# A two-layer encoder: all sums of the rope pairs' second-level product on VectorE instead of GpSimd, its inner products in two groups, single units spread between the pairs

## The chip, the cores and the metric

The kernel runs on one core of a Trainium2 chip. The metric is the device time of one execution in microseconds (us), the median of several runs. An engine here is one of TensorE (PE; its weight loads are listed apart as PEld), VectorE (DVE), ScalarE (ACT), GpSimd (POOL) and SyncE (SP), which only issues DMAs. Each engine works through its own queue in order and waits for the others by semaphores.

## What is computed

Two requests of 512 tokens by 1024 channels each go through the same two layers, in float32. Layer 1 is differential attention, layer 2 bidirectional retention; each has one wide input projection (8192 columns in layer 1, 6144 in layer 2), of which the queries and keys are rotated in pairs of columns ("rope"), the values are taken as they are, and a gate goes through SiLU; an output projection ends the layer. Cut to what matters here:

```
def diff_attention(h, w_in, ..., w_out, lambda_init):
    proj = h @ w_in
    q, k, v, gate = jnp.split(proj, [DA_QK_WIDTH, 2 * DA_QK_WIDTH, 2 * DA_QK_WIDTH + D_INNER], axis=-1)
    q = rotary_half(q.reshape(B, S, 2 * N_HEADS, DA_HEAD_DIM)) * (DA_HEAD_DIM ** -0.5)
    k = rotary_half(k.reshape(B, S, 2 * N_HEADS, DA_HEAD_DIM))
    ...
    o = rms_norm(o, subln_g, SUBLN_EPS) * (1.0 - lambda_init)
    o = o.reshape(B, S, D_INNER) * jax.nn.silu(gate)
    return o @ w_out

def trunk(x, ...):
    for i in range(DEPTH):          # 2: attention, then retention
        h = rms_norm(x, norm_g[i], NORM_EPS)
        x = x + (diff_attention(h, ...) if i % 2 == 0 else bidir_retention(h, ...))
    return rms_norm(x, final_norm_g, NORM_EPS)
```

The change touches only the input projections `h @ w_in` of both layers.

## The kernel before

**Split products.** Each operand is split into a high part (a cast on ScalarE, helper `hi_of`, L439) and a low part (a subtraction on VectorE, helper `lo_of`, L442); a product of two operands takes three passes of matmuls (`PASSES`). In the rows of the profile a split of `st` into `ws` is thus one ACT CAST at L439 and one DVE TENSOR_TENSOR at L442.

**Units.** The projection is cut into units of 256 columns, seen as two column halves, two halves of the 1024 input channels, and the two requests. A unit's 2 x 2 x 2 block product is done with seven products P1 to P7 (a Winograd scheme): sums of weight blocks (`combine`, L648) times sums of blocks of the input (`Bop`: B11, B21, B22, T1 to T4, made once per layer by `make_b`). One product is twelve matmuls of 128 x 512 at L712. Results are summed out of PSUM banks (`evac`, sums at L773, copies at L765). A "rope pair" unit is followed by the rotation (`rot_done`); gates are units too, and the values come as "wide" units of twice the width (L722), which hold two `pj` banks and split their last result straight out of them (`os<-pj` at L442). `pj` has three banks.

**Duos.** Two rope units u and v that follow each other share their P2, the product with B21: a `Duo` does it by a second level of the same scheme, over quarter blocks. It has seven inner products of six matmuls of 128 x 256 each (`inner`, L870), into two banks of tag `o`: `yv` and `yu`. Its weight sums s1 to s4 (`put`, L818) and its sums out of the banks (`kept`, L880, behind a ScalarE copy at L879; `added` at L884) are 256 or 512 columns wide. It has four steps, D0 to D3, each with one operand tile in the ring `ws`; the ring has six places, and operands are made ahead as far as the places reach (`projections`). The sums of B21's quarters (`inner_blocks`, L534: t1, t2, t4, t3) are made once per layer. There are twelve duos, eight in layer 1 and four in layer 2.

**Order.** `product_order` lists the products: for a duo, P1 of u, the last product (`tail`) of the unit before, P1 of v, D0, P5 of u, D1, P6, D2, P3, D3, P7, then v's. `mixed` lists the units: two rope units, then a share of the single ones (wides and gates). In layer 1 it makes, after five gates, RR w RR g RR w RR w RR w RR RR RR and two gates, where RR is a duo's two units, w a wide and g a gate. The program is first recorded as operations; `Plan.arrange` then gives each engine its order from estimated costs, and `Plan.issue` writes it out. On the chip that order is fixed.

Of the kernel before, what the change touches and what calls it, by code (L numbers as in the profile page):

```python
# [13 lines left out]
ALU = mybir.AluOpType  # L14
# [3 lines left out]
S = 512  # L18
# [243 lines left out]
def trunk_kernel(  # L262
# [224 lines left out]
    def make_b(layer, source):  # L487
# [37 lines left out]
        def inner_blocks(h):  # L525
# [5 lines left out]
            def block(name, pairs, tile):  # L531
                x = tile
                for j, (a, b) in enumerate(pairs):
                    pool(256, lambda j=j, a=a, b=b: nc.gpsimd.tensor_tensor(x[:, j], a[0](), b[0](), op=ALU.subtract),  # L534
                         [a[1], b[1]], [(x, j)])
                if name != "t3":
                    stored(name, x)
# [52 lines left out]
        for k in range(4):  # L590
            sub(h21[k], h21[k], t[k])
            split("T4", k, *h21[k])
            yield
# [198 lines left out]
    class Duo:  # L792


        n_ws, wide, early = 1, False, None
        STEPS = ("D0", "D1", "D2", "D3")
# [13 lines left out]
        def prep(self, op):  # L810
            u, v = self.u, self.v
# [4 lines left out]
            def put(x, at, a, b, fn, r):  # L816
                out = lambda: four(x[:, at * 256:at * 256 + 256])
                pool(256, lambda: nc.gpsimd.tensor_tensor(out(), a(), b(), op=fn), r, [(x, at)])  # L818
                return out
# [33 lines left out]
        def inner(self, op, n, ps, c0, block, start):  # L853
# [19 lines left out]
            pe(0.681, fn, [w, *bt], [ps])  # L873

        def product(self, op):
            u, v = self.u, self.v

            def kept(e, c, ps, lo, c1):
                act(256, lambda: nc.scalar.copy(e[:, c:c + 256], ps[:, lo:lo + 256]), [ps], [(e, c)])  # L879
                pool(256, lambda: nc.gpsimd.tensor_tensor(  # L880
                    e[:, c:c + 256], e[:, c:c + 256], c1[:, c:c + 256], op=ALU.add), [(e, c), c1], [(e, c)])
# [124 lines left out]
    duos = [0]  # L1006

    def product_order(units, n):
# [14 lines left out]
        duos[0] = 0  # L1023
        while left:
            u = left.pop(0)
            v = left[0] if left else None
            if v and u.kind == v.kind == "pair" and u.done.__qualname__ == v.done.__qualname__:
                left.pop(0)
                d = Duo(u, v)
                duos[0] += 1  # L1030
                out += [(u, "P1"), tail, (v, "P1"), (d, "D0"), (u, "P5"), (d, "D1"), (u, "P6"), (d, "D2"), (u, "P3"),
                        (d, "D3"), (u, "P7"), (v, "P5"), (u, "P4"), (v, "P6"), (v, "P3"), (v, "P7")]
# [191 lines left out]
    def mixed(ropes, gates, wides, n, n_gates):  # L1224
# [173 lines left out]
    step(proj, 7 * len(first_units) + 2 * duos[0] - 6 - 60 - 4)  # L1398
# [201 lines left out]
    step(proj, 7 * len(second_units) + 2 * duos[0] - 10 - 3 - 14)  # L1600
# [270 lines left out]
```

## Time and profile before

| what | value |
|---|---|
| median of 3 runs | 1810.12 us (1809.93 to 1813.53) |
| the profiled execution | 1809.57 us |
| its span, first to last instruction | 1807.8 us |
| granted TensorE clock in it | 0.999 |
| busy share of TensorE / VectorE / ScalarE / GpSimd | 99% / 85% / 51% / 14% |
| HBM traffic | 181 GB/s over the span |

The page gives one line per group of instructions: line, engine, operation, what it writes and reads by the program's names, shape and count, then busy time and mean duration, then the idle time of the engine ahead of it and what ended it. TensorE, VectorE and the rest run beside each other, so a busy share is no bound by itself; the waits of TensorE say where it stood still. By time, the input projection of layer 1 lies between about 45 and 625 us, attention up to 1030, the input projection of layer 2 between about 1110 and 1500, and retention to the end.

### The profile page before, as it was taken

How to read it: one execution, taken by the hardware profiler on the slowest of the kernel's cores; microseconds unless marked ns; L12 is line 12 of the kernel's file. 1: busy time of each engine (PE TensorE's matmuls, PEld its weight loads, DVE VectorE, ACT ScalarE, POOL GpSimd, SP SyncE). 2: the span in 40 equal slices, each digit the busy share in tenths (PEclk: the TensorE clock that was granted, in tenths of full speed). 3: DMA queues.
4: the chain of work that ended last, by engine and by line, in shares of the span. 5: the costliest groups of instructions: out<-in, count | busy, mean ns of one | idle time of the engine just before them, and what ended most of it. 6: DMA issues, size and time to landing. Idle time of an engine off the chain costs nothing.

```text
span 1807.8 us, 28903 instructions
## 1 busy us (share of the span) xinstructions
PE 1781.4 (99%) x10533; PEld 1570.2 (87%) x10533; DVE 1538.0 (85%) x2535; ACT 924.6 (51%) x1988; POOL 245.8 (14%) x356
## 2 busy tenths in 40 slices
PE   9999999999999999999999999999999999999998
PEld 7789889898987888888888878898989998888887
DVE  8978798888799888888888898887988977888887
ACT  8664354444444565554555776444444355444446
POOL 1110110100126011111111211001001000111114
PEclk9999999999999999999999999999999999999999
DMA  6336455463645595544454514473646569664652
GB/s 217 113 112 202 145 174 159 139 195 117 210 121 171 168 350 215 187 187 166 164 188 147 187 65 158 129 233 106 234 133 229 162 203 405 239 239 175 234 209 94
DMA packets 162823, 328.89 MB, mean 182 GB/s; under 512 B 12772, under 2 KB 76920, under 8 KB 162680
## 3 DMA queue, kind: packets, MB, share of 16 engines
q1 hardware_dynamic: 162352, 326.71, 53.1%
q8 instruction: 82, 1.34, 0.3%
q14 instruction: 61, 0.50, 0.1%
q10 hardware_dynamic: 328, 0.34, 0.1%
HBM read 209.55 MB, written 117.44 MB: 181 GB/s over the span
## 4 chain that ended last, share of the span: by engine, by line
PE 85%; DVE 7%; DMA 2%; POOL 2%; issue 1%; ACT 1%; SPq 1%; POOLq 0%; DVEq 0%; ACTq 0%
PE pj L1159 19%; PE pj L712 17%; PE sc L712 10%; PE pj L722 8%; PE o L1487 5%; PE sc L1426 5%; PE o L712 4%; PE sc L722 4%; PE o L870 3%; PE o L1696 2%; PE o L722 2%; DVE ws L442 2%; PE sc L1652 1%; PE tp L1676 1%; PE o L1704 1%
## 5 line engine op out<-in xcount | busy, mean ns | idle before, releaser
L1159 PE MATMUL pj<-ws,arena 128*128 128x512 f32 x1542 | 377.9, 392 | 0.0
L1159 PEld LDWEIGHTS pj<-ws,arena 128*128 128x128 f32 x1542 | 281.8, 188 | 54.6 <-DVE m L988 0.3
L712 PE MATMUL pj<-b,ws 128*128 128x512 f32 x1080 | 263.5, 392 | 1.3 <-DVE b L442 0.7
L439 ACT CAST ws<-st 128x512 fp32r<-128x512 f32 (+1 forms) x260 | 153.3, 601 | 167.1 <-PE o L870 47.5
L712 PEld LDWEIGHTS pj<-b,ws 128*128 128x128 f32 x1080 | 199.4, 188 | 42.2 <-DVE b L442 1.1
L1164 DVE SCALAR_TENSOR_TENSOR b<-pj,pad,b 128x512 f32<-128x512 f32 (+1 forms) x257 | 191.1, 745 | 27.4 <-PE pj L1159 24.3
L442 DVE TENSOR_TENSOR ws<-st,ws 128x512 fp32r<-128x512 f32 (+1 forms) x260 | 176.9, 691 | 41.9 <-ACT ws L439 41.4
L712 PE MATMUL sc<-arena,ws 128*128 128x512 f32 x768 | 186.2, 391 | 0.0
L442 DVE TENSOR_TENSOR ws<-raw,ws 128x512 fp32r<-128x512 f32 (+2 forms) x177 | 143.1, 816 | 31.3 <-ACT ws L439 26.9
L712 PEld LDWEIGHTS sc<-arena,ws 128*128 128x128 f32 x768 | 141.5, 188 | 28.0
L712 PE MATMUL pj<-arena,ws 128*128 128x512 f32 x636 | 156.9, 391 | 7.4 <-DVE os L442 7.4
L712 PEld LDWEIGHTS pj<-arena,ws 128*128 128x128 f32 x636 | 118.1, 188 | 33.2 <-DVE os L442 8.5
L439 ACT CAST ws<-raw 128x512 fp32r<-128x512 f32 (+2 forms) x177 | 124.5, 715 | 29.6 <-PE pj L712 10.3
L1444 ACT ACTIVATE b<-sc,pad 128x512 f32<-128x512 f32 x128 | 87.4, 691 | 72.0 <-DVE pad L1434 71.8
L722 PE MATMUL pj<-ws,b 128*128 128x256 f32 x960 | 116.9, 275 | 0.0
L722 PEld LDWEIGHTS pj<-ws,b 128*128 128x128 f32 x960 | 113.3, 188 | 0.6
L765 ACT COPY c<-pj 128x512 f32<-128x512 f32 x104 | 60.9, 586 | 100.4 <-PE pj L712 62.3
L712 PE MATMUL o<-arena,ws 128*128 128x512 f32 x456 | 108.5, 390 | 3.0 <-DVE b L502 1.8
L712 PEld LDWEIGHTS o<-arena,ws 128*128 128x128 f32 x456 | 85.1, 188 | 21.0 <-ACT ws L439 2.0
L1426 PE MATMUL sc<-arena 128*128 128x512 f32 x384 | 102.0, 398 | 0.7 <-ACT b L1444 0.7
L439 ACT CAST os<-e 128x512 fp32r<-128x512 f32 x96 | 59.1, 621 | 79.6 <-DVE e L773 29.6
L1487 PEld LDWEIGHTS o<-arena 128*128 128x128 f32 x768 | 93.0, 188 | 2.5
(258 smaller groups left out, 3179.0 us busy)
## 6 DMA issues: line engine op xcount, KB each, us to landing
qk<-os SPq DMA_DIRECT2D x192, 256.0 KB, 3.5
arena<-qk SPq DMA_DIRECT2D x96, 512.0 KB, 6.6
v<-os SPq DMA_DIRECT2D x64, 512.0 KB, 4.8
arena<-v SPq DMA_DIRECT2D x64, 512.0 KB, 4.1
raw<-in_da_w_in_dram SPq DMA_DIRECT2D x63, 512.0 KB, 4.2
raw<-in_ret_w_in_dram SPq DMA_DIRECT2D x48, 512.0 KB, 4.3
os<-g SPq DMA_DIRECT2D x32, 512.0 KB, 7.6
g<-e SPq DMA_DIRECT2D x48, 256.0 KB, 3.8
```

What stands on the lines that cost most here:

```text
L439: act(n, lambda: nc.scalar.copy(dst(), src()), r, w)
L442: dve(n, lambda: nc.vector.tensor_tensor(dst(), src(), hi().bitcast(F32), op=ALU.subtract), r, w)
L712: nc.tensor.matmul(ps.t, a[u][0]()[:, k, :], bt[k][:, v, :], start=(opens and k == 0 and i == 0), stop=(k == 3 and i == 2), skip_group_che ...
L722: nc.tensor.matmul(ps[:, (t % 2) * 256:(t % 2) * 256 + 256], bt[k][:, v, t * P:(t + 1) * P], a[u][0]()[:, k, :], start=(opens and t % 2 == ...
L765: act(S, lambda c=c, ps=ps: nc.scalar.copy(c.t, ps.t), [ps], [c])
L870: nc.tensor.matmul(ps[:, c0:c0 + 256], w[:, lo:lo + P], of(b, j), start=(start and j == 0 and i == 0), stop=(j == 1 and i == 2), skip_grou ...
L1159: nc.tensor.matmul(ps[:, here], o[a][:, e, t * P:(t + 1) * P], u[b][:, e, here], start=(m == 0), stop=(m == 5))
L1164: axpy(n, lambda half=half, here=here, ps=ps: nc.vector.scalar_tensor_tensor(half, ps[:, here], rr[:, t % 2:t % 2 + 1], half, op0=ALU.mult ...
L1426: nc.tensor.matmul(s.t, q[:, a, t * P:(t + 1) * P], k[:, b, :], start=(n == 0), stop=(n == 2))
L1444: act(840, lambda j=j, s=s, m=m: nc.scalar.activation(p[:, j, :], s.t, AF.Exp, bias=m.t, accum_out=sm[:, 2 * j + n:2 * j + n + 1]), [s, m] ...
L1487: nc.tensor.matmul(o[:, e * 256:(e + 1) * 256], v[b][:, j, e * P:(e + 1) * P], aT[a][:, j, :], start=(n == 0), stop=(n % 12 == 11), skip_g ...
L1696: nc.tensor.matmul(o[:, e * 256:(e + 1) * 256], v_[v][:, 2 * c + j, e * P:(e + 1) * P], a_[:, u, j * 256:(j + 1) * 256], start=(e == 0 and ...
```

## The change

All second-level sums go from GpSimd to VectorE: the quarter sums of `inner_blocks`, the weight sums `put`, and `kept`, which now adds straight out of the bank instead of a ScalarE copy and a GpSimd sum. T4 is written to the tiles `t` instead of over `h21`, which the quarter sums read. A duo's four steps become two, D1 (with D0's two products) and D3 (with D2's), each taking two places of the ring, D3's group with t3 ahead of b22. The number of single units between the pairs is rounded on the running sum: layer 1 becomes RR w RR g RR RR w RR w RR RR w RR and two gates; layer 2 keeps its order.

```
             def block(name, pairs, tile):
...
-                    pool(256, lambda j=j, a=a, b=b: nc.gpsimd.tensor_tensor(x[:, j], a[0](), b[0](), op=ALU.subtract),
+                    dve(256, lambda j=j, a=a, b=b: nc.vector.tensor_tensor(x[:, j], a[0](), b[0](), op=ALU.subtract),
                          [a[1], b[1]], [(x, j)])
...
         for k in range(4):
-            sub(h21[k], h21[k], t[k])
-            split("T4", k, *h21[k])
+            sub(t[k], h21[k], t[k])
+            split("T4", k, *t[k])
...
     class Duo:
-        n_ws, wide, early = 1, False, None
-        STEPS = ("D0", "D1", "D2", "D3")
+        n_ws, wide, early = 2, False, None
...
         def prep(self, op):
+
+            for part in (("D0", "D1"), ("D2", "D3"))[op == "D3"]:
+                self.part(part)
+
+        def part(self, op):
...
             def put(x, at, a, b, fn, r):
-                pool(256, lambda: nc.gpsimd.tensor_tensor(out(), a(), b(), op=fn), r, [(x, at)])
+                dve(256, lambda: nc.vector.tensor_tensor(out(), a(), b(), op=fn), r, [(x, at)])
...
             def kept(e, c, ps, lo, c1):
-                act(256, lambda: nc.scalar.copy(e[:, c:c + 256], ps[:, lo:lo + 256]), [ps], [(e, c)])
-                pool(256, lambda: nc.gpsimd.tensor_tensor(
-                    e[:, c:c + 256], e[:, c:c + 256], c1[:, c:c + 256], op=ALU.add), [(e, c), c1], [(e, c)])
+                dve(256, lambda: nc.vector.tensor_tensor(
+                    e[:, c:c + 256], ps[:, lo:lo + 256], c1[:, c:c + 256], op=ALU.add), [ps, c1], [(e, c)])
...
-            if op == "D0":
+            if op == "D1":
                 self.yv, self.yu = bank("o"), bank("o")
                 self.eu, self.ev = e_t(), e_t()
-                self.inner(op, 0, self.yv, 0, "b11", True)
+                self.inner("D0", 0, self.yv, 0, "b11", True)
                 kept(self.eu, 0, self.yv, 0, u.s["c1"][0])
-                self.inner(op, 1, self.yu, 0, "b21", True)
-            elif op == "D1":
+                self.inner("D0", 1, self.yu, 0, "b21", True)
                 self.inner(op, 0, self.yu, 256, "t1", False)
                 kept(self.ev, 256, self.yu, 256, v.s["c1"][0])
                 self.inner(op, 1, self.yv, 0, "t2", False)
                 kept(self.eu, 256, self.yv, 0, u.s["c1"][0])
-            elif op == "D2":
-                self.inner(op, 0, self.yu, 256, "b22", False)
-                added(S, self.eu, 0, self.yu, 0, self.eu)
-                u.done(0, 0, [self.eu], u.s, False)
             else:
                 self.inner(op, 0, self.yv, 0, "t3", False)
                 added(256, self.ev, 256, self.yv, 0, self.ev)
+                self.inner("D2", 0, self.yu, 256, "b22", False)
+                added(S, self.eu, 0, self.yu, 0, self.eu)
+                u.done(0, 0, [self.eu], u.s, False)
                 self.inner(op, 1, self.yv, 0, "t4", False)
...
-                out += [(u, "P1"), tail, (v, "P1"), (d, "D0"), (u, "P5"), (d, "D1"), (u, "P6"), (d, "D2"), (u, "P3"),
-                        (d, "D3"), (u, "P7"), (v, "P5"), (u, "P4"), (v, "P6"), (v, "P3"), (v, "P7")]
+                out += [(u, "P1"), tail, (v, "P1"), (u, "P5"), (d, "D1"), (u, "P6"), (u, "P3"), (d, "D3"), (u, "P7"), (v, "P5"), (u, "P4"), (v, "P6"), (v, "P3"), (v, "P7")]
...
-        while ropes:
-            share = -(-len(others) // (len(ropes) // n))
-            out += ropes[:n] + others[:share]
-            ropes, others = ropes[n:], others[share:]
-        return out + others + end
+        groups, m = len(ropes) // n, len(others)
+        for k in range(groups):
+            share = -(-(k + 1) * m // groups) + (-k * m // groups)
+            out += ropes[k * n:(k + 1) * n] + [others.pop(0) for _ in range(share)]
+        return out + end
```

The rest of the diff follows from this: the counts of steps handed to `projections` lose the term for the duos, and the planner's cost of an inner product goes from 0.681 to 0.69.

**The boundary from a wide unit to the next pair.** VectorE's rows before, from the last sum of the second wide unit (L773) to the split out of its first `pj` bank; `raw` are weights as loaded, `st` sums of them, `ws` operands, `os` split results:

```order
L773 TENSOR_TENSOR e_1_516<-pj_2_411,c_1_521 128x512
L442 TENSOR_TENSOR ws_0_76<-raw_2_282,ws_0_76 128x256 x2
L442 TENSOR_TENSOR ws_1_78<-st_2_498,ws_1_78 128x512
L648 TENSOR_TENSOR st_0_475<-st_2_498,raw_0_266 128x512
L442 TENSOR_TENSOR os_2_614<-e_1_516,os_2_614 128x512
L648 TENSOR_TENSOR st_2_498<-raw_2_282,st_0_475 128x512
L442 TENSOR_TENSOR ws_2_80<-st_3_527,ws_2_80 128x512
L648 TENSOR_TENSOR st_3_527<-raw_0_266 128x512
L442 TENSOR_TENSOR os_0_359<-pj_1_365,os_0_359 128x512
```

In the change the same stretch, of which the first two rows, the sum at L773 and a split `ws<-st` of 512 columns, are left out here (L822 is `put`):

```order
L442 TENSOR_TENSOR ws_5_86<-raw_2_282,ws_5_86 128x256
L822 TENSOR_TENSOR st_1_490<-raw_3_292 128x256
L442 TENSOR_TENSOR ws_5_86<-raw_2_282,ws_5_86 128x256
L822 TENSOR_TENSOR st_1_490<-st_1_490,raw_2_282 128x256
L648 TENSOR_TENSOR st_2_498<-st_0_475,raw_0_266 128x512
L442 TENSOR_TENSOR os_1_362<-e_1_516,os_1_362 128x512
L442 TENSOR_TENSOR ws_0_76<-st_1_490,ws_0_76 128x512
L648 TENSOR_TENSOR st_3_527<-raw_2_282,st_2_498 128x512
L822 TENSOR_TENSOR st_0_475<-raw_2_282,st_1_490 128x256
L822 TENSOR_TENSOR st_0_475<-raw_2_282,raw_3_292 128x256
L648 TENSOR_TENSOR st_1_490<-raw_0_266 128x512
L442 TENSOR_TENSOR os_2_614<-pj_0_294,os_2_614 128x512
```

The four sums `put` now stand among the twelve rows ahead of the split out of the bank; before, eight instructions stood there.

**Inside a duo.** TensorE's rows before, from P1 of v on, at the first duo (`o_1` and `o_0` are the banks `yv` and `yu`; `sc` is a bank of P5 and P3):

```order
L712 MATMUL pj_2_411<-arena_75,ws_0_76 128x512 x12
L870 MATMUL o_1_333<-arena_75,ws_1_78 128x256 x6
L870 MATMUL o_0_306<-arena_75,ws_1_78 128x256 x6
L712 MATMUL sc_0_252<-arena_75,ws_2_80 128x512 x12
L870 MATMUL o_0_306<-b_22_709,ws_3_82 128x256 x6
L870 MATMUL o_1_333<-ws_6_88,ws_3_82 128x256 x6
```

and in the change:

```order
L712 MATMUL pj_2_411<-arena_75,ws_0_76 128x512 x12
L712 MATMUL sc_0_252<-arena_75,ws_1_78 128x512 x12
L874 MATMUL o_1_333<-arena_75,ws_2_80 128x256 x6
L874 MATMUL o_0_306<-arena_75,ws_2_80 128x256 x6
L874 MATMUL o_0_306<-b_22_926,ws_3_82 128x256 x6
L874 MATMUL o_1_333<-ws_6_88,ws_3_82 128x256 x6
```

P5 (`sc_0`) moved ahead of the group, so between the two products into `o_1` stand twelve matmuls of 256 columns, where six of those and twelve of 512 stood.

**T4 of layer 1.** VectorE's rows before, around the subtractions that make T4 (L516; `m` are the tiles `h21`, `b_24` to `b_27` the places of T4, `b_23` that of a quarter sum's low part):

```order
L442 TENSOR_TENSOR b_23_882<-e_0_246,b_23_882 128x512
L773 TENSOR_TENSOR e_4_648<-pj_2_411,c_2_546 128x512
L648 TENSOR_TENSOR st_3_527<-raw_0_266 128x512
L516 TENSOR_TENSOR m_1_441<-m_1_441,b_15_579 128x512
L516 TENSOR_TENSOR m_2_449<-m_2_449,b_15_579 128x512
L516 TENSOR_TENSOR m_3_470<-m_3_470,os_2_614 128x512
L516 TENSOR_TENSOR m_0_254<-m_0_254,os_2_614 128x512
L442 TENSOR_TENSOR b_24_911<-m_1_441,b_24_911 128x512
```

and in the change, where L534 is a quarter sum:

```order
L648 TENSOR_TENSOR st_0_475<-raw_0_266,raw_1_268 128x512
L534 TENSOR_TENSOR e_0_246<-m_1_441 128x256
L773 TENSOR_TENSOR e_1_516<-o_0_306,c_3_594 128x512
L442 TENSOR_TENSOR ws_0_76<-st_0_475,ws_0_76 128x512
L516 TENSOR_TENSOR b_15_579<-m_1_441,b_15_579 128x512
L516 TENSOR_TENSOR b_15_579<-m_2_449,b_15_579 128x512
L516 TENSOR_TENSOR os_2_614<-m_3_470,os_2_614 128x512
L516 TENSOR_TENSOR os_2_614<-m_0_254,os_2_614 128x512
L442 TENSOR_TENSOR ws_1_78<-raw_2_282,ws_1_78 128x512
L773 TENSOR_TENSOR e_2_544<-o_1_333,c_0_500 128x512
L442 TENSOR_TENSOR b_24_836<-b_15_579,b_24_836 128x512
```

T4 now stands ahead of all quarter sums but the first, and behind one of the four sums at L773 that it stood behind before.

More of the change, by code (lines that the diff above doesn't have):

```diff
@@ L872, in fn @@
                                          skip_group_check=True)
-            pe(0.681, fn, [w, *bt], [ps])
+            pe(0.69, fn, [w, *bt], [ps])
         def product(self, op):
@@ L1004, in v_done @@
         return done
-    duos = [0]
     def product_order(units, n):
@@ L1022, in product_order @@
         left = list(units[n:-1])
-        duos[0] = 0
         while left:
@@ L1396, in trunk_kernel @@
     act(32, lambda: nc.scalar.activation(powers.t, powers.t, AF.Exp), [powers], [powers])
-    step(proj, 7 * len(first_units) + 2 * duos[0] - 6 - 60 - 4)
+    step(proj, 7 * len(first_units) - 6 - 60 - 4)
     tiles = [(h, g, t) for h in range(NH) for g in range(NG) for t in range(NT)]
@@ L1599, in trunk_kernel @@
     plan.lands = 2.0
-    step(proj, 7 * len(second_units) + 2 * duos[0] - 10 - 3 - 14)
+    step(proj, 7 * len(second_units) - 10 - 3 - 14)
     plan.lands = 4.0
```

1 line of the change is left out of this document (removed).

## The prediction

> **What bounds the kernel now.** I read the page first, then the waits of TensorE alone, then the timeline around each of them. The page has the span and each engine's busy time:
>
> ```profile
> span 1807.8 us, 28903 instructions
> PE 1781.4 (99%) x10533; PEld 1570.2 (87%) x10533; DVE 1538.0 (85%) x2535; ACT 924.6 (51%) x1988; POOL 245.8 (14%) x356
> ```
>
> TensorE is busy for all but 26.4 us, and the change takes no matmul away. So it can win only what TensorE now waits. The view of the waits names who ended each wait of TensorE (us in total, times, longest):
>
> ```profile
> PE pj L712 <- DVE os L442: 7.4, 6, 1.7
> PE o L870 <- DVE e L884: 2.9, 2, 1.4
> ...
> PE pj L712 <- DVE b L442: 0.7, 1, 0.7
> ```
>
> These three rows, 11.0 us in nine waits, are the ones this change can reach: the others of that view stand in the start-up, where layer 2's input is turned, at the first softmax, and once, for 0.6 us, behind a gate's sum. The first row is the boundary from a wide unit to the next pair: the pair's P1 needs a `pj` bank, and the bank comes free with the split `os<-pj` on VectorE. The second is inside the duo, the third is where T4 of layer 1 is made.
>
> The timeline at the longest of the six boundary waits (start us, duration us, engine, line, operation; in brackets the idle time ahead and what ended it):
>
> ```profile
> 324.87 0.68 DVE L773 TENSOR_TENSOR e<-pj,c 128x512 f32<-128x512 f32 x1
> ...
> 325.80 1.01 POOL L818 TENSOR_TENSOR st<-raw 128x256 f32<-128x256 f32 x1 [59.96 <-DMA raw<-in_da_w_in_dram]
> 326.14 1.23 DVE L442 TENSOR_TENSOR ws<-st,ws 128x512 fp32r<-128x512 f32 x1
> ...
> 326.89 1.08 POOL L818 TENSOR_TENSOR st<-st,raw 128x256 f32<-128x256 f32 x1
> 327.29 1.23 DVE L648 TENSOR_TENSOR st<-st,raw 128x512 f32<-128x512 f32 x1
> ...
> 328.05 1.07 POOL L818 TENSOR_TENSOR st<-raw,st 128x256 f32<-128x256 f32 x1
> 328.44 1.23 DVE L442 TENSOR_TENSOR os<-e,os 128x512 fp32r<-128x512 f32 x1
> 328.53 0.58 ACT L439 CAST os<-pj 128x512 fp32r<-128x512 f32 x1
> 329.08 1.18 POOL L818 TENSOR_TENSOR st<-raw,raw 128x256 f32<-128x256 f32 x1
> 329.59 1.23 DVE L648 TENSOR_TENSOR st<-raw,st 128x512 f32<-128x512 f32 x1
> ...
> 332.13 0.68 DVE L442 TENSOR_TENSOR os<-pj,os 128x512 fp32r<-128x512 f32 x1
> ...
> 332.87 3.02 PE L712 MATMUL pj<-arena,ws 128*128 128x512 f32 x12 [1.71 <-DVE os L442]
> ```
>
> Four GpSimd sums run from 325.80 to 330.26, and the four VectorE instructions beside them take 1.23 us each, where the same form takes 0.68: 4 x 0.55 = 2.2 us lost. The cast that `os<-pj` needs was done at 329.11, so VectorE's queue alone was late, not ScalarE.
>
> Inside the duo the harm goes the other way:
>
> ```profile
> 535.95 8.02 POOL L880 TENSOR_TENSOR e<-e,c 128x256 f32<-128x256 f32 x2 [3.85 <-ACT e L879]
> ...
> 544.00 0.69 DVE L884 TENSOR_TENSOR e<-o,e 128x512 f32<-128x512 f32 x1 [1.32 <-POOL e L880]
> ...
> 545.68 0.98 PE L870 MATMUL o<-b,ws 128*128 128x256 f32 x6 [1.42 <-DVE e L884]
> ```
>
> VectorE has work without a break there, two GpSimd sums need 8.02 us, VectorE waits for them, TensorE for VectorE. By the second row of the waits only two of the twelve duos do this.
>
> **The change part by part.** The sums that move are these groups of GpSimd (count | busy us, mean ns), with the ScalarE copy that goes away and the VectorE form that is nearest to the new sum out of a bank:
>
> ```profile
> L880 POOL TENSOR_TENSOR e<-e,c 128x256 f32<-128x256 f32 x36 | 50.1, 1406 | 123.6 <-ACT e L879 118.5 <-DVE st L648 5.1
> L818 POOL TENSOR_TENSOR st<-raw,st 128x256 f32<-128x256 f32 x12 | 17.2, 1431 | 0.9
> L818 POOL TENSOR_TENSOR st<-raw,raw 128x256 f32<-128x256 f32 x12 | 16.1, 1341 | 0.0
> L818 POOL TENSOR_TENSOR st<-raw 128x256 f32<-128x256 f32 x12 | 13.4, 1114 | 587.2 <-DMA raw<-in_da_w_in_dram 346.4 <-DMA raw<-in_ret_w_in_dram 202.9 <-issue 38.0
> L818 POOL TENSOR_TENSOR st<-st,raw 128x256 f32<-128x256 f32 x12 | 12.8, 1066 | 0.9
> L534 POOL TENSOR_TENSOR e<-m,e 128x256 f32<-128x256 f32 x8 | 9.9, 1253 | 73.8 <-ACT e L990 36.9 <-DVE b L442 33.6 <-DVE ws L442 3.3
> L879 ACT COPY e<-o 128x256 f32<-128x256 f32 x36 | 13.4, 374 | 0.2
> L884 DVE TENSOR_TENSOR e<-o,c 128x256 f32<-128x256 f32 x12 | 5.1, 423 | 0.2
> ```
>
> 36 + 48 sums of the duos and 8 per layer of the inner blocks make 100 instructions of 256 columns. What one costs VectorE is the step from its start to the next start:
>
> ```profile
> 527.34 0.68 DVE L925 TENSOR_TENSOR e<-e,sin 128x512 f32<-128x512 f32 x1
> 527.94 0.68 DVE L925 TENSOR_TENSOR e<-e,cos 128x512 f32<-128x512 f32 x1
> ...
> 536.25 0.41 DVE L442 TENSOR_TENSOR ws<-st,ws 128x256 fp32r<-128x256 f32 x1
> ...
> 536.58 0.68 DVE L648 TENSOR_TENSOR st<-raw,raw 128x512 f32<-128x512 f32 x1
> ```
>
> 0.60 us for 512 columns, 0.33 for 256. So VectorE takes on 100 x 0.33 = 33 us. Where a duo's four sums slow four instructions, as above, they cost it 2.2 us today, against 4 x 0.33 = 1.3 on its own queue.
>
> *Wide to pair, -6.2 us.* Today 332.13 - 324.87 - 0.60 = 6.66 us lie between the last sum and `os<-pj`. In the order of the change six instructions of 512 and six of 256 stand there: 6 x 0.60 + 6 x 0.33 = 5.58 us. `os<-pj` comes 1.08 us earlier. The same twelve stand at each of the six boundaries that waits today. The six waits have a mean of 7.4 / 6 = 1.23 us; less 1.08 each, and with those that fall below zero cut at zero, I leave 1.2 us in all. Bounds: all 7.4 go, or, if the queue ahead of the last sum is late by as much as it gains, none.
>
> *Duo, -2.9 us.* With no GpSimd sum left in the chain the two waits lose their cause. What is late next is the new sum `kept`, which reads the bank itself: the second product into the same bank (t2) has to wait until it is done. Between them stand twelve matmuls now. How late VectorE reads a duo's bank is in these rows:
>
> ```profile
> 499.75 0.51 PE L870 MATMUL o<-arena,ws 128*128 128x256 f32 x3
> ...
> 500.37 0.69 DVE L884 TENSOR_TENSOR e<-o,e 128x512 f32<-128x512 f32 x1 [0.81 <-PE o L870]
> ...
> 502.83 0.87 PE L870 MATMUL o<-b,ws 128*128 128x256 f32 x6
> ...
> 504.24 0.42 DVE L884 TENSOR_TENSOR e<-o,e 128x256 f32<-128x256 f32 x1
> ```
>
> 0.11 us after the end at 500.26, having idled 0.81; 0.54 after the end at 503.70. A matmul steps (0.87 - 0.51) / 3 = 0.12 us, twelve 1.44, and some 1.3 us are left from the end of the first product. `kept` needs 0.11 + 0.42 + 0.06 (332.81 to 332.87 above) = 0.59 us, with the later of the two starts 1.02. Both fit. I charge 1.0 us for all new waits, between 0 and the 2.9 us that the waits of this product have now.
>
> *T4 of layer 1, -0.7 us.*
>
> ```profile
> 75.37 1.82 DVE L516 TENSOR_TENSOR m<-m,b 128x512 f32<-128x512 f32 x2
> ...
> 79.05 8.22 PE L712 MATMUL pj<-b,ws 128*128 128x512 f32 x35 [0.69 <-DVE b L442]
> ```
>
> T4 overwrites the tiles that the GpSimd sums still read; in the change it has its own target and stands ahead of nearly all those sums. Bounds 0 and 0.7. The eight sums put 2.6 us on a VectorE that is full here; what they delay are operands of duos that come tens of us later. If that cover is gone, 2.6 us are lost.
>
> *Edits at nothing.* ScalarE loses 13.4 us at 51% busy. A duo's operands take two of six places in the ring twice instead of one place four times; the products they wait on are the same. The spread takes the three neighbouring pairs at the end of layer 1 apart, to two runs of two; layer 2 keeps its order. It matters only if VectorE is the bound there. TensorE needs for a duo and its two units 144 matmuls of 512, in steps that this row of the chain gives, and 42 of 256:
>
> ```profile
> 142.23 5.44 PE pj L712 x24
> ```
>
> 144 x 5.44 / 24 = 32.6, and 42 x 0.12 = 5.0: 37.7 us. In the order of the change 51 rows of 512 and 12 of 256 stand on VectorE from one duo's first `kept` to the next one's where two pairs are neighbours: 51 x 0.60 + 12 x 0.33 = 34.6 us. It fits.
>
> **The sum.** -6.2 - 2.9 - 0.7 + 1.0 = -8.8 us on the profiled execution's 1809.57 us (1.77 beside its span): 1800.8. The median of the runs is 1810.12, 0.55 above; so 1801.3.
>
> **A rule of the notes against the row.** The slowed rows lose 0.55 us beside a GpSimd sum of 1.07. The Trainium skill (SBUF — State Buffer, Who interferes with whom) says that a VectorE instruction with two SBUF inputs and a GpSimd instruction that reads SBUF exclude each other, and the later one is blocked for the whole of the earlier. By that a sum would cost VectorE 1.07, four 4.3 us, and with them gone the boundary waits would vanish: 1.2 us less, an estimate of 1800.1. The trace shows half of that loss, so the forecast keeps 0.55.
>
> **The rivals.** *VectorE stays as late as before* (0.13). The 33 us that it takes on undo what it gets back, since some GpSimd sums cost it nothing today (beside the 8.02 us above it kept its 0.68), and the boundaries keep their waits: only 2.9 + 0.7 go, and 1.0 comes: 1807.5. For it: the 85% busy; against it: 5.58 against 6.66 us, counted at the very place.
>
> *The bank is read too late* (0.12; slower). `kept` is one more instruction in VectorE's queue, t2 follows after 1.3 us, and behind t2 stands everything TensorE has. A start later than 0.7 us is paid in full, twelve times. As late as 2.5 us, which is how far 544.00 lies behind its products, costs 12 x 1.8 = 21.6: about 1822. It ends on the slower side once a start is later than 0.7 + (9.8 + 3.6) / 12 = 1.8 us. Against it: VectorE idles 0.81 ahead of the ordinary read.
>
> *VectorE as the bound of neighbouring pairs* (in the 0.12, at most 0.02). If an instruction held the queue for its whole duration, 51 x 0.68 + 12 x 0.42 = 39.7 us would stand against 37.7, and 2 us per duo would come back, 24 in all, in place of the 1.0: about 1824. The Trainium skill (VectorE: DVE Perf Modes, The DRAIN you can't avoid) has such a rule: the next instruction waits until the pipe is empty. The starts 0.60 apart at 0.68 us each say otherwise.
>
> **How the numbers follow.** Forecast 0.75, the first rival 0.13, the slower ones 0.12. All 11.0 us gone and no new wait would be 1799.1. The weight loads, which start ahead of their matmuls, show the same waits longer:
>
> ```profile
> PEld pj L712 <- DVE os L442: 8.5, 6, 1.9
> ```
>
> 8.5 for 7.4 us; at that ratio 11.0 are 12.6, so the low end is 1797.5. High 1809.5 takes in the first rival and the mildest of the second. A measurement here tells 0.2% (3.6 us) from no change: faster means below 1806.5. Of the first rival all but its best counts as the same. Faster 0.75, same 0.13, slower 0.12.
>
> **What would show it.** Right: no 256-column row on GpSimd (its busy time falls by 50.1 + 59.5 + 9.9 = 119.5 us and a little, to below 126), VectorE at 2635 instructions and about the same busy time, no 1.23 us rows in the projections, `PE pj <- DVE os` at 1.2 us in all, no wait of the duo's product on `e`. Wrong: waits of the duo's product on the new `kept` row (the second rival), or boundary waits as long as now (the first).

## The result and the profile after

| | before | changed kernel |
|---|---|---|
| median of four runs, us | 1810.36 (1809.93 to 1813.53) | 1796.08 (1795.55 to 1796.32) |
| the profiled execution, us | 1809.57 | 1796.09 |
| its span, us | 1807.8 | 1794.1 |

The ratio is 0.9917, with a 95% interval from 0.99 to 0.9934. The change wins 14.3 us; about 9 were forecast, and the time lies below the low end of the range. First the engines of the changed kernel, as the page lists them, and the one new kind of row, `kept` on VectorE (L883):

```profile
span 1794.1 us, 28748 instructions
PE 1778.4 (99%) x10533; PEld 1569.9 (88%) x10533; DVE 1532.6 (85%) x2635; ACT 917.8 (51%) x1952; POOL 120.6 (7%) x256
L883 DVE TENSOR_TENSOR e<-o,c 128x256 f32<-128x256 f32 x36 | 15.1, 420 | 19.8 <-PE o L874 19.8
```

VectorE has 100 instructions more (2535 to 2635) and is busy 5.4 us less: the busy time that the sums brought, the rows that no longer lie beside a GpSimd sum gave back. `kept` waited for TensorE and for nothing else. The waits of TensorE, in us in total, times, longest:

```profile
PE pj L712 <- DVE os L442: 1.9, 3, 0.8
PE o L712 <- DVE b L502: 1.8, 1, 1.8
PE o L712 <- DVE arena L502: 1.2, 1, 1.2
```

Six boundary waits of 7.4 us have become three of 1.9. The duo's wait on `e` (2.9), the one on `b` (0.7), the one behind a gate's sum (0.6) and the one at the first softmax (0.7) have no row any more, and no row is new in the projections. A boundary of the changed kernel, start and duration of each row (compare the one at 324.87 to 332.87 before):

```profile
360.02 0.68 DVE L773 TENSOR_TENSOR e<-pj,c 128x512 f32<-128x512 f32 x1
...
361.56 0.42 DVE L822 TENSOR_TENSOR st<-raw 128x256 f32<-128x256 f32 x1
...
362.57 0.69 DVE L648 TENSOR_TENSOR st<-st,raw 128x512 f32<-128x512 f32 x1
363.17 0.69 DVE L442 TENSOR_TENSOR os<-e,os 128x512 fp32r<-128x512 f32 x1
...
366.25 0.69 DVE L442 TENSOR_TENSOR os<-pj,os 128x512 fp32r<-128x512 f32 x1
366.99 3.02 PE L712 MATMUL pj<-arena,ws 128*128 128x512 f32 x12 [0.69 <-DVE os L442]
```

No row takes 1.23 us. Of VectorE's additions, subtractions and products of 512 columns (TENSOR_TENSOR) that the timeline shows singly, 55 took over 0.9 us in the kernel before, each of them beside a GpSimd instruction; in the changed kernel none does. From the last sum to the split out of the bank it is 6.23 us, where it was 332.13 - 324.87 = 7.26: 1.03 us earlier, 1.08 were counted.

To see where the time went, both spans are cut where TensorE has done equal work. Each row is a stretch, its length, TensorE's busy time and its matmuls. Before:

```profile
74.00:96.10 22.10, 20.82 (x91) 1.00 0.50 164
96.10:588.90 492.80, 484.83 (x2958) 1.00 0.51 157
588.90:672.60 83.70, 83.02 (x416) 1.00 0.74 259
672.60:1261.00 588.40, 585.94 (x3317) 1.00 0.48 165
1261.00:1421.20 160.20, 157.94 (x1084) 1.00 0.57 186
1421.20:1807.80 386.60, 379.00 (x2341) 1.00 0.61 223
```

and the changed kernel:

```profile
74.00:94.30 20.30, 20.30 (x91) 1.00 0.52 159
94.30:580.30 486.00, 484.10 (x2959) 1.00 0.52 162
580.30:662.80 82.50, 82.47 (x416) 1.00 0.75 254
662.80:1251.30 588.50, 586.04 (x3318) 1.00 0.48 166
1251.30:1408.50 157.20, 157.20 (x1084) 1.00 0.59 190
1408.50:1794.10 385.60, 378.96 (x2341) 0.99 0.61 224
```

| stretch | forecast, us | measured, us |
|---|---|---|
| the rest of `make_b` of layer 1 | -0.7 | -1.8 |
| layer 1's pairs and layer 2's pairs | -8.1 (boundaries -6.2, duo -2.9, new waits +1.0) | -6.8 - 3.0 = -9.8 |
| start of attention | 0 | -1.2 |
| attention to the turning of layer 2's input | 0 | +0.1 |
| the rest, retention and the end | 0 | -1.0 |
| sum | -8.8 | -13.7 |

### The profile page after: what moved, and what is told of

Its sections match the earlier page's. It is cut to its first block, busy times and chain, and to the rows that moved or that the text cites. A ratio compares the mean times of both kernels' runs of the same rounds, so it can differ in the third digit from the quotient of the medians.

```text
span 1794.1 us, 28748 instructions
## 1 busy us (share of the span) xinstructions
PE 1778.4 (99%) x10533; PEld 1569.9 (88%) x10533; DVE 1532.6 (85%) x2635; ACT 917.8 (51%) x1952; POOL 120.6 (7%) x256
## 4 chain that ended last, share of the span: by engine, by line
PE 89%; DVE 6%; DMA 2%; issue 1%; ACT 1%; SPq 1%; POOL 0%; DVEq 0%; POOLq 0%; ACTq 0%
PE pj L712 20%; PE pj L1155 19%; PE sc L712 11%; PE pj L722 6%; PE o L712 5%; PE o L1483 5%; PE sc L1422 5%; PE o L874 3%; PE sc L722 3%; PE o L1692 2%; PE o L722 2%; DVE ws L442 1%; PE sc L1648 1%; PE tp L1672 1%; PE o L1700 1%
## 5 line engine op out<-in xcount | busy, mean ns | idle before, releaser
L712 PE MATMUL pj<-b,ws 128*128 128x512 f32 x1080 | 263.1, 391 | 0.0
L712 PEld LDWEIGHTS pj<-b,ws 128*128 128x128 f32 x1080 | 199.5, 188 | 39.8
L442 DVE TENSOR_TENSOR ws<-st,ws 128x512 fp32r<-128x512 f32 (+1 forms) x260 | 169.0, 662 | 28.1 <-ACT ws L439 26.4
L712 PE MATMUL sc<-arena,ws 128*128 128x512 f32 x768 | 185.8, 390 | 0.0
L442 DVE TENSOR_TENSOR ws<-raw,ws 128x512 fp32r<-128x512 f32 (+2 forms) x177 | 139.8, 798 | 34.8 <-ACT ws L439 30.5
L712 PEld LDWEIGHTS sc<-arena,ws 128*128 128x128 f32 x768 | 143.1, 188 | 29.5
L712 PE MATMUL pj<-arena,ws 128*128 128x512 f32 x636 | 156.8, 391 | 1.9 <-DVE os L442 1.9
L712 PEld LDWEIGHTS pj<-arena,ws 128*128 128x128 f32 x636 | 118.1, 188 | 27.5 <-DVE os L442 2.7
L712 PE MATMUL o<-arena,ws 128*128 128x512 f32 x456 | 108.6, 390 | 3.0 <-DVE b L502 1.8
L712 PEld LDWEIGHTS o<-arena,ws 128*128 128x128 f32 x456 | 85.1, 188 | 21.1 <-ACT ws L439 2.0
```

The source lines that it names most:

```text
L442: dve(n, lambda: nc.vector.tensor_tensor(dst(), src(), hi().bitcast(F32), op=ALU.subtract), r, w)
L712: nc.tensor.matmul(ps.t, a[u][0]()[:, k, :], bt[k][:, v, :], start=(opens and k == 0 and i == 0), stop=(k == 3 and i == 2), skip_group_che ...
```

## The experiments

Two theories stood after the result. **Company**: a GpSimd sum slows the VectorE instruction that runs beside it, and this alone made the bank, the duo's sums and T4 late. **Order**: the two groups of inner products, T4's own target and the spread of the single units moved what TensorE waits for. The first set takes single parts out of the changed kernel, the second puts single parts into the kernel before, the third measures company by itself. Each ratio is to the kernel before, timed beside it on the same chip. A difference between two rows of the table is taken across chips, on which the medians of the kernel before lie between 1809.82 and 1810.83 us; less than about 1 us between two rows says little.

| run | median, us | ratio, 95% interval |
|---|---|---|
| changed kernel | 1796.08 | 0.9917 (0.99 to 0.9934) |
| `put` back on GpSimd | 1804.85 | 0.9972 (0.9963 to 0.9981) |
| `kept` back on ScalarE and GpSimd | 1797.63 | 0.9935 (0.9922 to 0.9947) |
| quarter sums back on GpSimd | 1802.38 | 0.9953 (0.9939 to 0.9966) |
| old spread | 1796.99 | 0.9932 (0.9918 to 0.9945) |
| old target of T4 | 1796.78 | 0.9923 (0.991 to 0.9935) |
| four steps instead of two | 1796.92 | 0.9927 (0.9915 to 0.994) |
| before, `put` alone on VectorE | 1799.62 | 0.9944 (0.9932 to 0.9957) |
| before, `kept` alone on VectorE | 1806.48 | 0.9981 (0.9972 to 0.999) |
| before, quarter sums alone on VectorE | 1807.10 | 0.9986 (0.9977 to 0.9996) |
| changed, with idle sums on GpSimd | 1815.22 | 1.0032 (1.002 to 1.0043) |
| changed, with idle fills on GpSimd | 1796.66 | 0.9926 (0.9914 to 0.9939) |
| changed, P5 ahead of v's P1 | 1793.53 | 0.9905 (0.9891 to 0.9918) |

### Parts taken out of the changed kernel

**The weight sums.**

```
-                dve(256, lambda: nc.vector.tensor_tensor(out(), a(), b(), op=fn), r, [(x, at)])
+                pool(256, lambda: nc.gpsimd.tensor_tensor(out(), a(), b(), op=fn), r, [(x, at)])
```

> The changed kernel with the 48 weight sums `put` back on GpSimd; all else as changed. If the sums beside VectorE's own work made the bank come late (0.55 us lost by each VectorE instruction that runs beside one, against 0.33 us on its own queue), the split out of the bank comes some 0.9 us later at each wide-to-pair boundary: the waits of TensorE on the split `os` at L442 grow from 1.9 us to 5 to 7, rows of 1.23 us stand beside the GpSimd sums again, and the time is 1800 to 1802. If the order in two groups or the new spread brought the boundary gain, the waits stay near 1.9 us and the time within 1 us of 1796.1.

It measured 1804.85 us, 8.8 above the changed kernel. The waits of TensorE in this run:

```profile
PE pj L712 <- DVE os L442: 7.7, 6, 1.8
...
PE o L874 <- DVE e L883: 1.2, 2, 0.6
```

All six boundary waits are back though groups and spread are new. The second row is not the wait of before: two duo products wait for `kept` on VectorE, as the second rival had it. Company holds here, order falls. The size was put too low: these two rows are 7.0 us more than in the changed kernel, not 3 to 5.

**`kept`.**

```
-                dve(256, lambda: nc.vector.tensor_tensor(
-                    e[:, c:c + 256], ps[:, lo:lo + 256], c1[:, c:c + 256], op=ALU.add), [ps, c1], [(e, c)])
+                act(256, lambda: nc.scalar.copy(e[:, c:c + 256], ps[:, lo:lo + 256]), [ps], [(e, c)])
+                pool(256, lambda: nc.gpsimd.tensor_tensor(
+                    e[:, c:c + 256], e[:, c:c + 256], c1[:, c:c + 256], op=ALU.add), [(e, c), c1], [(e, c)])
```

> The changed kernel with the 36 sums `kept` back as a ScalarE copy and a GpSimd sum; all else as changed. If a full VectorE starves GpSimd and the duo then waits for its sum, some wait of a duo's product on `e` comes back where two pairs are neighbours, with GpSimd rows of several us: 1.5 to 3 us in all, 1797.5 to 1799. If the grouping or the spread removed these waits (the products that need the bank next come later), no such wait is seen and the time stays within 0.7 us of 1796.1. The waits at the wide-to-pair boundaries stay near 1.9 us by both.

It measured 1797.63 us. In its waits no duo's product waits for `e`; the boundaries have 2.5 us, and one row is back that has nothing to do with the duos:

```profile
PE pj L712 <- DVE os L442: 2.5, 4, 1.0
...
PE sc L1423 <- ACT b L1441: 0.7, 1, 0.7
```

That is the wait at the first softmax. The time fell into the first theory's band, but not by its mechanism: `kept` on GpSimd makes no duo wait here. Which part of the change prevents it the run does not say: `put` is gone from GpSimd, but in the new groups VectorE's sum that frees the duo's bank also stands ahead of the one that reads GpSimd's (307.37 and 310.71 us at a neighbouring pair). More on this order below.

**The quarter sums.**

```
-                    dve(256, lambda j=j, a=a, b=b: nc.vector.tensor_tensor(x[:, j], a[0](), b[0](), op=ALU.subtract),
+                    pool(256, lambda j=j, a=a, b=b: nc.gpsimd.tensor_tensor(x[:, j], a[0](), b[0](), op=ALU.subtract),
```

> The changed kernel with the 16 quarter sums of the inner blocks back on GpSimd and T4 still in its own tiles. If the 1.8 us won by 90 us come from GpSimd's company there (eight sums, 0.55 us each, 4.4 us on a full VectorE against 2.6 us of its own), half or more comes back: 1797 to 1798, with waits at 79 and 90 us. If they come from T4's own target alone, nothing moves: 1796.1 within 0.4.

It measured 1802.38 us, 6.3 above the changed kernel: far more than expected. Layer 1's wait behind a gate's sum is back (`PE pj L712 <- DVE e L773`, 1.0 us, at 92 us), though T4 has its own target. The larger part is at layer 2's `make_b`, where neither kernel waits:

```profile
1091.26 1.23 DVE L442 TENSOR_TENSOR ws<-st,ws 128x512 fp32r<-128x512 f32 x1
1092.41 1.22 DVE L442 TENSOR_TENSOR ws<-raw,ws 128x512 fp32r<-128x512 f32 x1
...
1098.36 0.68 DVE L648 TENSOR_TENSOR st<-raw,raw 128x512 f32<-128x512 f32 x1
1099.13 0.62 ACT L439 CAST ws<-st 128x512 fp32r<-128x512 f32 x1 [0.56 <-DVE st L648]
1099.79 4.57 PE L712 MATMUL pj<-b,ws 128*128 128x512 f32 x12 [2.03 <-ACT ws L439]
```

TensorE waits 2.03 us for a cast of a late weight sum, and the twelve matmuls behind it take 4.57 us where twelve take 2.88. The planner also ordered ScalarE's rows differently here, so this place is not a clean undoing, and what share company has in it stays open.

**The old spread.** The loop of before in `mixed` (its removed lines in the diff above) takes the place of the new one.

> The changed kernel with the old rounding of the single units: three neighbouring pairs at the end of layer 1's projection. If VectorE has slack in neighbouring pairs (34.6 us of starts against 37.7 us of TensorE per duo) the spread is worth nothing: within 0.7 us of 1796.1, no wait of a duo's product. If the spread took part of the duo's waits away, one or two waits of 1 us or more on `e` or on the bank stand between 500 and 610 us: 1797.5 to 1800.

It measured 1796.99 us, with boundary waits of 2.2 us in four and no wait of a duo's product, though three pairs are neighbours again. Of the 0.9 us, a wait of 0.4 at the first softmax has a row. The spread is worth nothing that these runs can tell.

**The old target of T4.**

```
-            sub(t[k], h21[k], t[k])
-            split("T4", k, *t[k])
+            sub(h21[k], h21[k], t[k])
+            split("T4", k, *h21[k])
```

> The changed kernel with T4 of layer 1 written over the tiles h21 again, behind the quarter sums, which are VectorE's now. If T4's place behind the GpSimd sums was what cost 0.85 and 0.75 us where T4 is made and behind the gate's sum near 90 us, it comes back in part, since eight VectorE sums of 0.33 us stand ahead of T4: 1796.5 to 1797.5, with the waits at about 79 us seen again. If only GpSimd's company cost that time, nothing moves: 1796.1 within 0.4.

It measured 1796.78 us (1795.14 to 1798.69), and the waits on `b` at 79 us and on the gate's sum at 90 us are not back. T4's own target wins nothing that is seen.

**Four steps.** The kernel before with all sums on VectorE, the new T4 target and the new spread, but D0 to D3 one by one.

> The kernel before with all sums on VectorE, the new T4 target and the new spread, but with the duo's four steps: only the grouping of the change is missing. If the grouping was needed, it is because t2 follows the first product into its bank sooner: waits of a duo's product on the sum `kept` at the bank, up to 12 x 0.5 us, and 1797 to 1802. If the engine of the sums brought everything, the time is within 1 us of 1796.1.

It measured 1796.92 us, with no wait of a duo's product. Within the intervals the two groups bring nothing; `kept` is in time in both forms.

### Parts put into the kernel before

**`put` alone on VectorE** (the diff of the first experiment, turned round).

> The kernel before with the 48 weight sums `put` alone on VectorE; everything else as before. Putting them back into the changed kernel cost 8.8 us and brought the boundary waits back. If their company on GpSimd is the main cause, they are worth as much here: boundary waits on `os` from 7.4 to about 2 us, 1801 to 1803.5 against 1810.5 before. Open is the wait of the duo's product on `e` (2.9 us before): it goes too if VectorE's lost time fed it, and stays if the GpSimd sum `kept` in its chain made it.

It measured 1799.62 us, below what was expected: 10.6 of the 14.3 us by this line alone. Its boundary waits, beside which there is no duo row:

```profile
PE pj L712 <- DVE os L442: 2.8, 5, 0.9
```

The duo's wait is gone although `kept` is still on GpSimd and is still starved:

```profile
531.66 7.77 POOL L880 TENSOR_TENSOR e<-e,c 128x256 f32<-128x256 f32 x2 [3.58 <-ACT e L879]
```

Two sums take 7.77 us, and nobody waits. Before it was 8.02 us with a wait. But the planner also turned two sums of VectorE round here. Before, the sum of 512 columns that reads GpSimd's and waits for it (544.00) stood ahead of the sum of 256 columns that frees the bank:

```profile
545.21 0.41 DVE L884 TENSOR_TENSOR e<-o,e 128x256 f32<-128x256 f32 x1
```

In this run it stands behind it:

```profile
538.78 0.42 DVE L884 TENSOR_TENSOR e<-o,e 128x256 f32<-128x256 f32 x1
...
545.05 0.68 DVE L884 TENSOR_TENSOR e<-o,e 128x512 f32<-128x512 f32 x1
```

The sum that frees the bank no longer waits for GpSimd. So this run does not show that a faster VectorE ended the duo's wait.

**`kept` alone on VectorE** (the second diff, turned round).

> The kernel before with the 36 sums `kept` alone on VectorE, out of the bank; everything else as before. As predicted the wait of the duo's product on `e` (2.9 us) goes and the boundary waits stay: 1807 to 1808 against 1810.5. If the sums `put` feed that wait instead, most of it stays, and the time is within 1 us of before.

It measured 1806.48 us, 3.7 below before. The duo's row is gone and the boundaries keep theirs (7.2 us in six). So the duo's wait goes with either move alone. But in both runs, and only in the two duos that waited before, VectorE's two sums are turned round (here 256 columns at 543.34 and 580.93, 512 columns at 545.48 and 586.40). The order alone makes no wait without a starved sum on GpSimd: ten duos of the kernel before have the same order of the two sums and no wait. Whether the moved sums or the turned order ended it, no run tells, since none has the old order without the starved sum in these duos.

**The quarter sums alone on VectorE** (the third diff, turned round; T4 still overwrites the tiles that they read).

> The kernel before with the 16 quarter sums alone on VectorE, T4 still written over the tiles they read; everything else as before. If GpSimd's company in that stretch cost the waits at 79 and 90 us, both go though T4's target is the old one: 1.5 to 2 us less, 1808.5 to 1809. If T4 needed its own target, T4 stays late and nothing is won.

It measured 1807.10 us (1805.65 to 1812.13), 3.1 below before; by the ratio's interval it is between 0.7 and 4.2. The row on `b` (0.7) is gone and that behind the gate's sum has fallen from 0.6 to 0.2; both duo waits are still there. Its profiled execution nevertheless has no shorter span than before, 1808.7 us. One boundary cost it 1.6 us more than its wait:

```profile
410.27 4.61 PE L712 MATMUL pj<-arena,ws 128*128 128x512 f32 x12 [1.79 <-DVE os L442]
```

Behind a wait of 1.79 us the twelve matmuls took 4.61 us instead of 3.02.

### Company by itself

**Idle sums.** Beside each `put` of VectorE, GpSimd makes the same sum once more, into a tile that nothing reads:

```
                 dve(256, lambda: nc.vector.tensor_tensor(out(), a(), b(), op=fn), r, [(x, at)])
+                idle = m_t([P, S])
+                pool(256, lambda: nc.gpsimd.tensor_tensor(four(idle[:, 0:256]), a(), b(), op=fn), r, [idle])
```

> The changed kernel, and beside each of the 48 weight sums of VectorE the same sum on GpSimd as well, into a tile that nothing reads. No chain passes through GpSimd, so only its company is added. If company alone slows VectorE (0.55 us by each instruction beside a sum), a duo's four sums cost VectorE 2.2 us: at the boundaries the split comes up to 2.2 us later, their waits grow from 1.9 to between 7 and 13 us, and the time is 1801 to 1807. If it was the latency of GpSimd's chain that delayed the operands, nothing moves: within 1 us of 1796.1.

It measured 1815.22 us, 19.1 above the changed kernel and slower than before. A boundary of this run:

```profile
366.59 1.12 POOL L824 TENSOR_TENSOR m<-raw,st 128x256 f32<-128x256 f32 x1 [0.36 <-DVE st L822]
367.04 1.23 DVE L442 TENSOR_TENSOR os<-e,os 128x512 fp32r<-128x512 f32 x1
367.68 1.19 POOL L824 TENSOR_TENSOR m<-raw,raw 128x256 f32<-128x256 f32 x1
368.19 1.23 DVE L442 TENSOR_TENSOR ws<-st,ws 128x512 fp32r<-128x512 f32 x1
...
371.94 4.41 PE L712 MATMUL pj<-arena,ws 128*128 128x512 f32 x12 [2.87 <-DVE os L442]
```

The rows of 1.23 us are back, beside sums that no one waits for, and the row of the boundary waits is 14.3 us in six, 12.4 more than in the changed kernel. Company is enough: between the last sum and the split out of the bank the same twelve VectorE rows stand as in the changed kernel, and they take 8.42 us (362.79 to 371.21) instead of 6.23, 2.19 us more, where 4 x 0.55 = 2.2 were expected. The other part is TensorE's busy time, 1785.0 for 1778.4 us, and most of it lies in one effect: three waits of more than 2.6 us are each followed by slow matmuls, as in the last row. That the expected 1801 to 1807 was too low comes from both.

**Idle fills.** The same place, and a GpSimd instruction that reads nothing:

```
+                idle = m_t([P, S])
+                pool(256, lambda: nc.gpsimd.memset(idle[:, 0:256], 0.0), r, [idle])
```

> The changed kernel, and beside each of the 48 weight sums of VectorE a GpSimd instruction that only writes 256 columns of zeros into a tile that nothing reads, where the run with idle sums also read two operands. If it is GpSimd's reading of SBUF that slows VectorE, the fills cost nothing: within 1 us of 1796.1, no row of 1.23 us. If any GpSimd instruction on SBUF slows it, or the tile taken from the ring of `m` does, a good part of the 19 us of the idle sums is seen: 1803 or more.

It measured 1796.66 us, within the changed kernel's interval. The 48 fills as a group, and one of them (330.77) beside VectorE:

```profile
L824 POOL MEMSET m<- 128x256 f32 x48 | 13.9, 313 | 821.2 <-DVE m L953 505.8 <-DVE os L442 125.7 <-ACT c L990 86.4
330.56 0.69 DVE L955 TENSOR_TENSOR e<-e,e 128x512 f32<-128x512 f32 x1
330.77 0.32 POOL L824 MEMSET m<- 128x256 f32 x1 [22.02 <-DVE m L953]
```

No row beside a fill is longer, and from the last sum to the split it is 6.21 or 6.22 us at five of the six boundaries, as in the changed kernel; one boundary wait of 1.90 us in its profiled execution has another cause, which stays open. The fills are not a full twin: they read no operand, so they run as soon as their tile is free, at other times than the sums, and for 0.31 us each. But the tile from the ring of `m` can be excluded as the cause of the 19 us. The Trainium skill (SBUF — State Buffer, Who interferes with whom) says that a VectorE instruction with two SBUF inputs contends with a GpSimd instruction that reads SBUF, not with one that only writes it. Both runs agree with that.

### A version that beats both

What is left at the boundary is P1 of v asking for the bank. Behind a wide unit, P5 of u, which goes to another bank, is put ahead of it:

```
-                out += [(u, "P1"), tail, (v, "P1"), (u, "P5"), (d, "D1"), (u, "P6"), (u, "P3"), (d, "D3"), (u, "P7"), (v, "P5"), (u, "P4"), (v, "P6"), (v, "P3"), (v, "P7")]
+                out += [(u, "P1"), tail, *([(u, "P5"), (v, "P1")] if tail[0].wide else [(v, "P1"), (u, "P5")]), (d, "D1"), (u, "P6"), (u, "P3"), (d, "D3"), (u, "P7"), (v, "P5"), (u, "P4"), (v, "P6"), (v, "P3"), (v, "P7")]
```

> The changed kernel with P5 of u ahead of P1 of v where the unit before is a wide one. The bank that P1 of v needs is asked for one product (2.7 us) later, and P5 goes to another bank. If the boundary waits that are left (three, up to 0.99 us) are all due to the split out of the bank, they vanish and nothing else changes: 1794, 2 us below the changed kernel. If P5's operand is not ready so early, its wait takes their place: 1796 to 1797.5.

It measured 1793.53 us (1793.09 to 1794.10). No wait on `os` at L442 is left among TensorE's rows; the first ones are those of the turning points:

```profile
PE o L712 <- DVE b L502: 1.8, 1, 1.8
PE o L712 <- DVE arena L502: 1.2, 1, 1.2
PE sc L1286 <- DVE pad L452: 1.2, 1, 1.2
```

That is 2.5 us below the changed kernel by medians. They were not timed side by side and the ratios' intervals overlap, but no run of the one reaches a run of the other.

## Why the prediction missed

The main mechanism held. What failed are terms of the sum: the new waits, the price of a wait, T4, and two places that were put at nothing.

- **What bounds it** held: TensorE's waits, reached through a VectorE slowed by GpSimd's sums. The idle-sums run shows this as the cause at the boundaries, where the same rows came 2.19 us later, and `put` is the main carrier.
- **The boundary term** (-6.2) held nearly: the split out of the bank came 1.03 us earlier, 1.08 were worked out, and 1.9 us of waits are left where I left 1.2. In idle time it is -5.5.
- **The duo term** (-2.9) held in size; its reason was incomplete. I put the wait down to the GpSimd sum in the duo's own chain. By the rows the wait ran through that starved sum and through VectorE's order, with the sum that reads it (544.00) ahead of the one that frees the bank (545.21). Both single moves that ended the wait turned that order round, and the groups of the change do so too, so the runs do not tell engine from order. The sum at 544.00 also reads the bank of an earlier product than I took: it lies 6.0 us behind that product's end (538.04), not 2.5, which I used to price the second rival.
- **New waits** (+1.0) were the first mis-sized term: they measured 0. `kept` waited 19.8 us for TensorE and was never waited for.
- **Waits were priced at TensorE's idle time**, and this is the second step that failed. In the two stretches of the pairs the idle time fell by (492.80 - 484.83) + (160.20 - 157.94) - (486.00 - 484.10) - 0 = 8.3 us, the stretches by 9.8. The busy time shrank with it though no matmul went. The row behind a wait is itself longer, 3.02 us for twelve matmuls where 2.88 is usual; that covers 0.14 us of each wait and not the whole 1.5. The waits of the weight loads come nearer. Before, behind their 8.5 us on `os`:

```profile
PEld o L870 <- DVE e L884: 3.7, 2, 1.9
```

  and in the changed kernel, with no such row on `e`:

```profile
PEld pj L712 <- DVE os L442: 2.7, 4, 1.0
```

  That is 8.5 + 3.7 - 2.7 = 9.5 us. I had seen that these waits are longer and used them for the low end only.
- **T4 of layer 1** (-0.7, bounds 0 and 0.7) was the third: the stretch lost 1.8 us. I had written the wait behind a gate's sum off as out of reach, and it stood on the same slowed VectorE. The reason was wrong too: T4's own target did nothing (with the old one in the changed kernel no wait is back), while quarter sums alone moved to VectorE end the wait on `b` with the old target. The bound 0.7 came from one row, not from the stretch.
- **The edits at nothing**: spread and groups are worth nothing that can be told, as said. But start of attention (-1.2) and the end (-1.0) were not at nothing. At the first the wait of 0.7 us on a ScalarE row is gone; it comes back in two variants whose edit lies elsewhere, and I take it for a matter of timing. The end lies behind the last matmul: from there to the end of the span it was 7.6 us before and 6.6 in the changed kernel. It is 6.6 to 6.7 in every other run but one (7.05 with the quarter sums back), whichever single part was moved, so no part of the change by itself is needed for it. The causes of both stay open.
- **The Trainium skill's rule** (SBUF — State Buffer, Who interferes with whom) of a block for the whole instruction I priced at a slowed sum's 1.07 us, and no such row lost so much: beside sums of 1.12 and 1.19 us the idle-sums run has rows of 1.23, that is 0.55 lost, as before. By that price the boundaries would have kept nothing; they kept 1.9 us. But a sum that starts ahead of its neighbour takes only 0.74 us there (363.94), and the row of 256 columns 0.05 us behind it takes 0.97 us instead of 0.42, again 0.55 lost. So the longer sums may hold a wait of their own, and the rule itself is not refuted, only the price that I gave it.
- **The range**: the missing 4.9 us are 1.1 at T4, 1.0 of new waits and 0.7 in the pairs beside them (1.5 behind the waits, less 0.7 too much at the boundaries and 0.1 of rounding), 1.2 and 1.0 at the two places counted at nothing, less 0.1 lost in attention. The low end of 1797.5 assumed that only three rows of waits could change. A change that speeds up VectorE in all stages of the projections can reach every wait that ends on it, and the bound belonged at the sum of those.

The rivals fell: VectorE did not stay late (1.9 us of boundary waits, not 7.4), no bank was read too late (with `put` back on GpSimd two were, for 1.2 us in all), and neighbouring pairs (old spread) showed no wait on VectorE.

## What to carry to other kernels

Moving a sum from GpSimd to VectorE can make VectorE faster where both read SBUF: count what the sum takes from its neighbours (0.55 us of each row beside it here) against what it costs in VectorE's own queue (0.33 us). Take the effect stretch by stretch, at equal work of the bounding engine, and price a wait from start to start, not by its idle time. Parts tried one by one need not add up: `put`, `kept` and the quarter sums alone won 10.6 + 3.7 + 3.1 = 17.4 us, together 14.3. The duo's wait of 2.9 us, which goes with either of two, is counted twice in that; the intervals of the ratios, about 2 us either way for each, are too wide to show more. And look at the order as well as the engine: moving one sum can make the planner turn others round.

## What the runs showed of the hardware

- A wait of about two microseconds can cost nearly twice its length. The clock, microsecond by microsecond, around the wait of 2.87 us in the idle-sums run (TensorE restarts at 371.94):

```profile
371.00:372.00 1.00, 0.06 (x1) 0.76 0.00 0
372.00:373.00 1.00, 1.00 (x3) 0.50 0.43 70
373.00:374.00 1.00, 1.00 (x4) 0.50 0.65 147
374.00:375.00 1.00, 1.00 (x4) 0.54 0.95 312
375.00:376.00 1.00, 1.00 (x6) 1.00 1.07 411
```

  The number behind the count (x1 to x6) is the granted clock: half speed for some three microseconds, and twelve matmuls take 1.4 us more (4.41 against 3.01 or 3.02). Waits of 2.63, 2.87 and 3.46 us in that run all did this. Of waits between 1.71 and 2.06 us in all the runs, 1.79 (quarter sums alone) and 2.03 (quarter sums back) did, and 1.71, 1.78, 1.82, 1.90 and 2.06 did not. So length alone does not decide. The Trainium skill (TensorE: Matmul & The Clock Gate, Part 1: The HAM clock gate) speaks of a free-running activity window of about 3.4 us, which would fit a chance by phase but is not shown by any run here, and of half rate after at least one idle window; here 1.79 us of standing still were enough.
- Where VectorE works without a break, two GpSimd sums of 256 columns took 7.77 us (`put` alone on VectorE), while the mean one takes 1.4 in the kernel before. GpSimd is slowed as well.
